# A head norm's four small transfers, moved from SyncE's queue to ScalarE's and GpSimd's

## The chip, the cores and the metric

The kernel runs on one core of a Trainium2 chip. The metric is the device time in microseconds of one execution; lower is better. Engines are named as the profile names them: PE (TensorE, the matrix multiplier; PEld is its weight load), DVE (VectorE), ACT (ScalarE), POOL (GpSimd) and SP (SyncE, which here only issues DMAs). An engine executes its instructions in the order in which they stand in its queue. A DMA is issued by an instruction in some engine's queue; if it has to wait for something, everything behind it in that queue waits too.

## What is computed

One layer of a hybrid decoder over 2048 tokens of width 1024, in float32. Two groups of token mixers run side by side on one input projection, their outputs go through one output projection, then a squared-ReLU MLP and a gated embedding follow. Cut to what matters here:

```python
def gated_head_norm(o, w, z):
    o = o * rsqrt(mean(o * o, axis=-1, keepdims=True) + EPS)
    return o * w * silu(z)

hn   = rms_norm(h, pre_mix_norm)
proj = einsum('btd,dc->btc', hn, w_in)
o_a  = gated_delta_rule_chunked(q_a, k_a, v_a, g_dec, beta)   # 4 heads of 128
o_a  = gated_head_norm(o_a, gdn_norm, z_gdn)
o_b  = hgrn2_chunked(silu(q_hg), k_b, i_hg, log_f)            # 4 heads of 128
o_b  = gated_head_norm(o_b, hgrn_norm, g_hg)
mix_out = einsum('btc,cd->btd', concat(o_a, o_b), w_out)
h = h + rms_norm(mix_out, post_mix_norm)
...   # MLP with its two norms, then the gated embedding
```

The change concerns `gated_head_norm`: 8 heads in each of 4 quarters of the tokens, 32 norms.

## The kernel before

Channels lie on the 128 partitions and tokens along the free axis, in quarters of 512 tokens (`QT`). A tile is `[128, 512]` float32. Weights and operands are split into two float32r parts, and a product is three matmuls.

**Order of the work.** The mixers are one loop over 132 `works` (for each quarter one product for the decays and 4 x 8 products for the heads). PE goes through them in the order in which the code is written (`manual_schedule` for PE), and so does SyncE within this loop. Each work is cut into 3 steps (`SPT`), and at each step a clock `tick()` resumes the generators that stand in an `agenda` at that step: `gdn_mixer` (the delta rule, names ending in `_g`) and `hgrn_mixer` (names ending in `_h`), one each per head. `A_STEPS` and `B_STEPS` are their lists of steps, counted from the head's first product; a head has 24 steps. The order on DVE, ACT and POOL in this part is not written out: the framework's planner sets it from the order of the code and from its own estimates of durations.

**The head norm.** Both mixers end in `finish`, which squares the head's output (`osq`), multiplies it by its gate (`og`) and calls `norm_steps`. This sums the squares over the partitions with two matmuls by a matrix of ones (L283, L284), so that each partition of a PSUM bank `nrm` holds all 512 sums. Then, in separate steps:

1. ACT copies one row of it (L286), and the row is stored to DRAM as `sd` (L288, 2 KB).
2. The row is loaded back as a block of 128 x 4, `m` (L291), so that the arithmetic is short.
3. DVE scales it (L293), POOL raises it to the power -0.5 (`rsqrt`, L172).
4. The block is stored to DRAM as `rd` (L297, 2 KB).
5. `spread_load` loads it, repeated on all partitions, as `rsb` (L257, 256 KB).
6. DVE multiplies `og` by the head's gain and `rsb` (L622), and `og` is stored to `mixd` (L624), from where the output projection's operands `mixT` are loaded (L341).

For the HGRN head these steps stand at 46, 48, 50, 52, 53, 54, 58 and 59 of `B_STEPS`, for the delta rule's head at 53, 55, 57, 59, 60, 61, 65 and 66 of `A_STEPS`. The last head of all has lists of its own (`A_LAST`, `B_LAST`).

All DMAs here are issued from SyncE. Its queue in the mixers also holds the weights: 512 KB raw loads and 1 MB stores to a cache in the first quarter, 1 MB loads from the cache afterwards (L197). Further, there are the delta rule's own round trips through DRAM (`ud` L709, `sys` L718, `xd` L752, `xn` L759, and `gf` L640), the squares of the next quarter's inputs (`xs` L495), and the MLP's weight sums (`wd` L1133, `sumd` L1144). POOL computes `rsqrt` for the norms, for the delta rule's keys (`rk`, on which DVE's L677 waits) and for the inputs, and clears `xn`. Its only DMAs are 16 that add the residual to the output projection's results (L1299), after the mixers.

`norm_steps` is also called for the embedding's norms (names ending in `_e`), and `spread_load` for others; these calls keep SyncE.

Of the kernel before, what the change touches and what calls it, by code (L numbers as in the profile page):

```python
# [20 lines left out]
P = 128  # L21
# [3 lines left out]
QT = 512  # L25
NQ = T // QT
NC = QT // P
# [69 lines left out]
def trunk(ctx, tc, x, xT, pT, vecs, w_in, w_ab, gdn_a_log, gdn_dt_bias, w_out, w_up, w_down,  # L97
          w_ple, w_gate, consts, out):
    nc = tc.nc
# [11 lines left out]
    def bank(name, pool=None):  # L111
        return (pool or pm).tile([P, QT], F32, tag="ps", name=name)
# [24 lines left out]
    def col(r):  # L137
        return cols[:, r : r + 1]
# [32 lines left out]
    def rsqrt(v):  # L171
        G.tensor_tensor(v, v, mhalf, ALU.pow)  # L172

    def split(t, eng, raw):

        S.activation(t[:, 0], raw, AF.Copy)  # L176
        eng.tensor_tensor(t[:, 1], raw, t[:, 0], ALU.subtract)  # L177
# [56 lines left out]
    def squares(acc, src, k, name, eng=V):  # L234

        if acc is None:
            acc = st.tile([P, QT], F32, tag="acc", name=f"acc_{name}", bufs=3)
            S.activation(acc, src, AF.Square)
        else:
            turns[0] += 1  # L240
            if pair[0] and turns[0] % 2:
                sq = st.tile([P, QT], F32, tag="late", name=f"sq_{name}_{k}")
            else:
                sq = st.tile([P, QT], F32, tag="sq", name=f"sq_{name}_{k}", bufs=1)
            S.activation(sq, src, AF.Square)  # L245
            eng.tensor_tensor(acc, acc, sq, ALU.add)  # L246
        return acc
# [4 lines left out]
        nc.sync.dma_start(rd.rearrange("o (p n) -> (o p) n", n=NC), m)  # L252
        return rd

    def spread_load(rd, name, pool=None, tag="rsb", bufs=2):
        rsb = (pool or st).tile([P, QT], F32, tag=tag, name=f"rsb_{name}", bufs=bufs)
        nc.sync.dma_start(rsb, rd.broadcast_to([P, QT]))  # L257
        return rsb

    def row_norm(acc, scale, eps, name):  # L260

        out = []
        for _ in norm_steps(acc, scale, eps, name, out.append):
            pass
        return out[0]
# [8 lines left out]
    yod = {q: [dr.tile([P, QT], F32, name=f"yod{q}_{d}") for d in range(KD)] for q in (0, 2, 3)}  # L274
    ple_r = [None] * NQ

    def norm_steps(acc, scale, eps, name, done, pool=None):

        hl = st.tile([P, 2, QT], F32R, tag="hl", name=f"hl_{name}", bufs=1)
        split(hl, V, acc)  # L280
        yield
        ps = bank(f"nrm_{name}", pool or pp)
        PE.matmul(ps, ones, hl[:, 0, :], start=True, stop=False)  # L283
        PE.matmul(ps, ones, hl[:, 1, :], start=False, stop=True)  # L284
        row = acc[0:1, :]
        S.activation(row, ps[0:1, :], AF.Copy)  # L286
        sd = dr.tile([1, QT], F32, name=f"sd_{name}")
        nc.sync.dma_start(sd, row)  # L288
        yield
        m = sm.tile([P, NC], F32, tag="m", name=f"m_{name}")  # L290
        nc.sync.dma_start(m, sd.rearrange("o (p n) -> (o p) n", n=NC))  # L291
        yield
        V.tensor_scalar(m, m, scale, eps, ALU.mult, ALU.add)  # L293
        rsqrt(m)
        yield
        rd = dr.tile([1, QT], F32, name=f"rd_{name}")
        nc.sync.dma_start(rd.rearrange("o (p n) -> (o p) n", n=NC), m)  # L297
        done(rd)

    def stage_ple(i, name):  # L300
# [91 lines left out]
    with ExitStack() as ectx:  # L392
        es = ectx.enter_context(tc.tile_pool(name="es", bufs=1))
        with tc.manual_schedule(engines={mybir.EngineType.SP, mybir.EngineType.Activation, mybir.EngineType.DVE}):
# [39 lines left out]
            ple[1] = ple1(V)  # L434
            x_r[0] = spread(ss, "x0")
            rsb = spread_load(x_r[0], "x0")
            load_xraw((4, 6))
            nc.sync.dma_start(cst[:, C_NEG:], consts[:, C_NEG:])
            done = []
# [23 lines left out]
    with mixers as mctx:  # L463
# [145 lines left out]
        def finish(q, h, pso, zt, extra, eps, n):  # L609

            og = st.tile([P, QT], F32, tag="late", name=f"og_{n}")
            sq = st.tile([P, QT], F32, tag="acc", name=f"osq_{n}", bufs=3)
            S.activation(sq, pso, AF.Square, scale=P ** -0.5)
            V.tensor_tensor(og, pso, zt, ALU.mult)
            if extra is not None:
                V.tensor_tensor(sq, sq, extra, ALU.add)
            rd = []
            yield from norm_steps(sq, 1.0, eps, n, rd.append)
            yield
            rsb = spread_load(rd[0], n)  # L620
            yield
            V.scalar_tensor_tensor(og, og, col(R_GNORM if h < 4 else R_HNORM), rsb, ALU.mult, ALU.mult)  # L622
            yield
            nc.sync.dma_start(mixd[q][h], og)  # L624
# [10 lines left out]
        def gdn_mixer(q, h, live):  # L635
# [181 lines left out]
            for c in range(NC):  # L817
# [20 lines left out]
                state[h] = s2  # L838
                yield
            yield from finish(q, h, pso, live.pop("z"), q2, EPS * EPS * P, n)  # L840

        def side(t, n, s, late):
# [17 lines left out]
        def hgrn_mixer(q, h, live):  # L860
# [101 lines left out]
            for c in range(NC):  # L962
# [4 lines left out]
                if c % 2:  # L967
                    yield
            yield from finish(q, 4 + h, pso, zt, None, EPS, n)


# [118 lines left out]
        def load_x(q):  # L1090

            rsb = spread_load(x_r[q], f"x{q}", m2, "rsx", 1)
            raws = {}

# [61 lines left out]
        for q in range(2):  # L1156
            at(0, norm_steps(accs[q], 1.0 / D, EPS, f"e{q}", partial(ple_r.__setitem__, q)),
               [4 * q + i for i in (0, 2, 4, 5, 6)])
# [302 lines left out]
    for j, (q, d) in enumerate(order):  # L1461
# [46 lines left out]
        acc = square_sums[q] = squares(square_sums[q], ps, d, f"o{q}")  # L1508
# [404 lines left out]
    rsb = {q: spread_load(ple_r[q], f"pg{q}", None, "acc", 3) for q in (0, 1)}  # L1913
    es, puts = {(q, 0): embedded(q, 0, rsb[q]) for q in (0, 1)}, []
    for half in range(2):
# [4 lines left out]
        for d in range(KD):  # L1920
# [4 lines left out]
            if d + 1 == KD and half == 0:  # L1925
                rsb = {q: spread_load(ple_r[q], f"pg{q}", None, "acc", 3) for q in (2, 3)}
# [65 lines left out]
```

## Time and profile before

| | |
|---|---|
| time, median of 3 runs | 2636.42 us (2636.26 to 2639.48) |
| the profiled execution: time, span | 2639.52 us, 2637.8 us |
| granted TensorE clock, mean | 0.999 |
| PE, PEld | 2602.5 us (99%), 2146.7 us (81%) |
| DVE, ACT, POOL | 1964.9 us (74%), 1464.5 us (56%), 137.7 us (5%) |
| DMA | 573.87 MB, mean 218 GB/s |
| DMA by queue, share of 16 engines | hardware queue 64.6%, software queue (POOL's) 1.0% |

A row of a group of instructions gives line, engine, operation, written tile <- read tiles, count, and durations (minimum/median/maximum in ns) or busy time. "A <- B: total, times, longest" is a wait: A's engine stood idle until B ended. `SPq` and `POOLq` are issues in these engines' queues; the time of an issue is the instruction's, not the transfer's. In a timeline a line begins with start and duration in us, and brackets give the idle time ahead of it and what ended it. The granted clock is a share of TensorE's full speed.

### The profile page before, as it was taken

The numbers are of one execution on the slowest core, as the hardware profiler recorded it, in microseconds if no ns is written. First come the engines' busy times: TensorE is split into PE (matmuls) and PEld (weight loads), VectorE is DVE, ScalarE is ACT, GpSimd is POOL, SyncE is SP. The second block draws the span as 40 slices with busy tenths as digits, with TensorE's granted clock in tenths as the row PEclk, the third lists the DMA queues.
The fourth block names the chain that finished last, engine by engine and source line by source line (L and its number), as shares of the span: only waits on it lengthen the run. The fifth ranks groups of instructions, "written<-read, shape, count | busy, mean of one in ns | idle before, by whom it ended". The sixth has DMA issues, their size and how long they took to land.

```text
span 2637.8 us, 43913 instructions
## 1 busy us (share of the span) xinstructions
PE 2602.5 (99%) x15593; PEld 2146.7 (81%) x15593; DVE 1964.9 (74%) x4032; ACT 1464.5 (56%) x2991; POOL 137.7 (5%) x147
## 2 busy tenths in 40 slices
PE   8999999999999999999999999999999999999999
PEld 6788888887878888877888888888888888888887
DVE  7778777776777777579988778767877765477776
ACT  7775655465556555566666455555455465565332
POOL 0000000000000000110000000001000001101000
PEclk9999999999999999999999999999999999999999
DMA  8877777767767675864675576665644375677663
GB/s 276 286 265 261 268 267 235 229 228 242 244 205 247 224 236 162 237 206 135 219 233 180 180 235 224 211 214 185 221 146 168 140 246 186 203 252 253 202 218 133
DMA packets 267788, 573.87 MB, mean 218 GB/s; under 512 B 55578, under 2 KB 60152, under 8 KB 250416
## 3 DMA queue, kind: packets, MB, share of 16 engines
q1 hardware_dynamic: 265264, 566.86, 64.6%
q0 software_dynamic: 2304, 4.20, 1.0%
q8 instruction: 123, 2.02, 0.3%
q14 instruction: 97, 0.79, 0.1%
HBM read 410.57 MB, written 160.37 MB: 216 GB/s over the span
## 4 chain that ended last, share of the span: by engine, by line
PE 68%; DVE 3%; DMA 3%; issue 2%; ACT 1%; SPq 0%; POOL 0%; DVEq 0%; ACTq 0%; POOLq 0%
PE d L1213 23%; PE u L1213 23%; PE mm L1179 9%; PE mmg L1213 7%; PE mmo L1062 1%; PE mme L203 1%; DMA yod<-yo 1%; DMA mixT<-mixd 0%; DVE t L177 0%; DVE acc_o L246 0%; DMA sys_g<-ud_g 0%; PE psc_g L832 0%; PE of_g L837 0%; PE of_g L836 0%; PE of_h L966 0%
## 5 line engine op out<-in xcount | busy, mean ns | idle before, releaser
L1179 PE MATMUL mm<-xt,w 128*128 128x512 f32 x3072 | 786.4, 401 | 1.2 <-DVE acc_vg L571 1.1
L1179 PEld LDWEIGHTS mm<-xt,w 128*128 128x128 f32 x3072 | 553.8, 189 | 107.4 <-issue 1.6
L1213 PE MATMUL d<-db,da 128*128 128x512 f32 x2688 | 612.9, 389 | 0.0
L1213 PE MATMUL u<-t,wu 128*128 128x512 f32 x2604 | 591.2, 389 | 0.0
L1213 PEld LDWEIGHTS d<-db,da 128*128 128x128 f32 x2688 | 504.5, 188 | 104.8
L1213 PEld LDWEIGHTS u<-t,wu 128*128 128x128 f32 x2604 | 488.7, 188 | 101.5
L230 DVE TENSOR_TENSOR db<-db 128x512 fp32r<-128x512 f32 x224 | 160.6, 717 | 58.2 <-ACT db L229 56.8
L1615 DVE TENSOR_TENSOR u<-u,u 128x512 f32<-128x512 f32 x224 | 150.4, 682 | 52.4 <-PE u L1213 50.9
L229 ACT ACTIVATE db<-db 128x512 fp32r<-128x512 f32 x224 | 141.0, 630 | 66.4 <-DMA db<-hid 62.0
L1213 PE MATMUL mmg<-h2T,wg 128*128 128x512 f32 (+1 forms) x792 | 174.7, 383 | 0.0
L1213 PEld LDWEIGHTS mmg<-h2T,wg 128*128 128x128 f32 x792 | 145.5, 188 | 29.1
L1658 ACT ACTIVATE u<-u 128x512 f32<-128x512 f32 x128 | 80.8, 631 | 153.2 <-DVE u L1615 152.2
L177 DVE TENSOR_TENSOR da<-da 128x512 fp32r<-128x512 f32 x128 | 94.1, 736 | 90.3 <-ACT da L176 88.3
L176 ACT ACTIVATE da<-da 128x512 fp32r<-128x512 f32 x128 | 80.7, 630 | 127.1 <-DMA da<-sumd 103.6
L1213 PE MATMUL mmo<-mixT,w_out 128*128 128x512 f32 x600 | 138.1, 390 | 2.7 <-DVE w_out L177 2.7
L1213 PEld LDWEIGHTS mmo<-mixT,w_out 128*128 128x128 f32 x600 | 112.3, 188 | 27.4 <-DVE w_out L177 4.0
L176 ACT ACTIVATE wu<-a 128x512 fp32r<-128x512 f32 x124 | 75.0, 623 | 54.5 <-DMA a<-in_w_up_dram 52.2
L177 DVE TENSOR_TENSOR wu<-a,wu 128x512 fp32r<-128x512 f32 x124 | 85.9, 695 | 7.9 <-ACT wu L176 7.5
L177 DVE TENSOR_TENSOR da<-dr,da 128x512 fp32r<-128x512 f32 x96 | 68.2, 711 | 23.6 <-ACT da L176 22.7
L1659 ACT ACTIVATE u<-u 128x512 f32<-128x512 f32 x128 | 80.4, 628 | 3.0
L246 POOL TENSOR_TENSOR acc_y<-acc_y,sq_y 128x512 f32<-128x512 f32 x28 | 38.5, 1375 | 758.9 <-ACT sq_y L245 758.9
L176 ACT ACTIVATE da<-dr 128x512 fp32r<-128x512 f32 x96 | 60.5, 630 | 28.9 <-DMA dr<-in_w_down_dram 23.9
(401 smaller groups left out, 3680.2 us busy)
## 6 DMA issues: line engine op xcount, KB each, us to landing
w<-cache_in SPq DMA_DIRECT2D x96, 1024.0 KB
db<-hid SPq DMA_DIRECT2D x224, 256.0 KB
cache_in<-w SPq DMA_DIRECT2D x32, 1024.0 KB
hid<-u SPq DMA_DIRECT2D x128, 256.0 KB
da<-sumd SPq DMA_DIRECT2D x128, 256.0 KB
a<-in_w_up_dram SPq DMA_DIRECT2D x124, 256.0 KB
hid<-ht SPq DMA_DIRECT2D x96, 256.0 KB
dr<-in_w_down_dram SPq DMA_DIRECT2D x96, 256.0 KB
```

The lines of the kernel that those rows point to most:

```text
L176: S.activation(t[:, 0], raw, AF.Copy)
L177: eng.tensor_tensor(t[:, 1], raw, t[:, 0], ALU.subtract)
L203: PE.matmul(ps, a, b, start=i == 0, stop=i == n - 1)
L229: S.activation(t[:, 0], plain(t), AF.Copy)
L230: V.tensor_tensor(t[:, 1], plain(t), t[:, 0], ALU.subtract)
L246: eng.tensor_tensor(acc, acc, sq, ALU.add)
L1062: PE.matmul(ps, w[:, term // 2, k, :], xin[q][k][:, term % 2, :], start=i == 0, stop=i == 3 * KD - 1)
L1179: PE.matmul(ps, *terms[i], start=i == 0, stop=i == nt - 1)
L1213: PE.matmul(ps, a, b, start=start, stop=stop)
L1615: V.tensor_tensor(c[new], c[old], ps, ALU.add)
L1658: S.activation(c[k], c[k], AF.Relu)
L1659: S.activation(c[k], c[k], AF.Square)
```

## The change

In the head norms of the mixers alone, four DMAs change their issuing engine: the row's store `sd` is issued by ScalarE, the block's load `m`, its store `rd` and the spread load `rsb` by GpSimd. Sizes, steps, buffers and arithmetic stay. Since ScalarE's and GpSimd's queues are ordered by the planner in this part, the place of these DMAs in their new queues is the planner's choice, while on SyncE it was the place in the code.

```diff
-    def spread_load(rd, name, pool=None, tag="rsb", bufs=2):
+    def spread_load(rd, name, pool=None, tag="rsb", bufs=2, queue=nc.sync):
         rsb = (pool or st).tile([P, QT], F32, tag=tag, name=f"rsb_{name}", bufs=bufs)
-        nc.sync.dma_start(rsb, rd.broadcast_to([P, QT]))
+        queue.dma_start(rsb, rd.broadcast_to([P, QT]))
         return rsb
...
-    def norm_steps(acc, scale, eps, name, done, pool=None):
-
+    def norm_steps(acc, scale, eps, name, done, pool=None, aside=False):
+
+        give, take = (nc.scalar, nc.gpsimd) if aside else (nc.sync, nc.sync)
...
         sd = dr.tile([1, QT], F32, name=f"sd_{name}")
-        nc.sync.dma_start(sd, row)
+        give.dma_start(sd, row)
         yield
         m = sm.tile([P, NC], F32, tag="m", name=f"m_{name}")
-        nc.sync.dma_start(m, sd.rearrange("o (p n) -> (o p) n", n=NC))
+        take.dma_start(m, sd.rearrange("o (p n) -> (o p) n", n=NC))
         yield
         V.tensor_scalar(m, m, scale, eps, ALU.mult, ALU.add)
         rsqrt(m)
         yield
         rd = dr.tile([1, QT], F32, name=f"rd_{name}")
-        nc.sync.dma_start(rd.rearrange("o (p n) -> (o p) n", n=NC), m)
+        take.dma_start(rd.rearrange("o (p n) -> (o p) n", n=NC), m)
         done(rd)
...
-            yield from norm_steps(sq, 1.0, eps, n, rd.append)
-            yield
-            rsb = spread_load(rd[0], n)
+            yield from norm_steps(sq, 1.0, eps, n, rd.append, aside=True)
+            yield
+            rsb = spread_load(rd[0], n, queue=nc.gpsimd)
```

## The prediction

> **What bounds the kernel now.** I read the page's busy times first, then the busy time by stretch, then who waited for whom, then the chain that ended last.
>
> ```profile
> span 2637.8 us, 43913 instructions
> PE 2602.5 (99%) x15593; PEld 2146.7 (81%) x15593; DVE 1964.9 (74%) x4032; ACT 1464.5 (56%) x2991; POOL 137.7 (5%) x147
> 90.00:1010.00 920.00, 909.49 (x7888) 752.24 (x7887) 700.90 (x2026) 531.75 (x1405) 53.10 (x61) 1.00 0.73 244
> 1010.00:1220.00 210.00, 202.19 (x1084) 164.81 (x1083) 151.73 (x255) 127.50 (x227) 18.71 (x20) 1.00 0.64 191
> ```
>
> The third and fourth lines are stretches: length, then busy us of PE, PEld, DVE, ACT and POOL, granted clock, DMA share, GB/s. TensorE is idle for 2637.8 - 2602.5 = 35.3 us in all. The changed norms run in the mixers (90 to 1010) and in the first part of the output projection (to 1093). There PE is idle for 920 - 909.5 = 10.5 us and 210 - 202.2 = 7.8 us. So 18.3 us, 0.7%, is all that a perfect result could remove, apart from what an idle stretch costs in clock afterwards.
>
> ```profile
> PE at_all L918 <- DVE acc_vg L572: 3.3, 1, 3.3
> PE mmo L1213 <- DVE w_out L177: 2.7, 3, 1.2
> 610.75 5.74 DMA rd_g<-m_g
> 616.56 4.56 DMA rsb_g<-rd_g
> 621.15 0.75 DVE og_g L622
> 624.05 1.10 PE at_all L918 x4
> 617.00 0.63 ACT L500 ACTIVATE xs<-xs 128x512 f32<-128x512 f32 x1 [2.01 <-DMA xs<-in_x_dram]
> 611.16 0.38 SPq L495 DMA_DIRECT2D xs<-in_x_dram  x1
> 620.00:625.00 5.00, 1.70 (x10) 1.46 (x9) 3.82 (x8) 1.33 (x4) 0.00 (x0) 0.91 1.01 393
> 625.00:630.00 5.00, 5.00 (x19) 4.01 (x19) 4.56 (x14) 2.24 (x5) 0.00 (x0) 0.74 0.65 202
> ```
>
> The first two lines are PE's waits (total, times, longest). The largest one in the mixers, 3.3 us before 624.05, is the end of a head norm: the chain's pieces (start, length) run through the norm's store rd_g, its spread load rsb_g and the multiplication L622, behind which the conv taps (acc_vg) stand on DVE. The ACT line shows a second delay just ahead of it: xs, issued on SyncE right after rd_g's store (611.16 behind 610.75), came 2.0 us late. The two stretches show the price after the gap: granted clocks of 0.91 and 0.74, which is 5 x 0.09 + 5 x 0.26 = 1.75 us.
>
> **The change part by part.** Per head norm four DMAs leave SyncE's queue: the row's store sd (to ScalarE), and the block's load m, its store rd and the spread load rsb (to GpSimd). There are 32 norms.
>
> ```profile
> L288 SPq DMA_DIRECT2D sd_h<-osq_h x16: 245/246/252, 156.6 to 1056.2; - x16
> L291 SPq DMA_DIRECT2D m_h<-sd_h x16: 319/322/1008, 161.3 to 1057.3; - x16
> L297 SPq DMA_DIRECT2D rd_h<-m_h x16: 319/332/463, 166.9 to 1061.7; - x16
> L257 SPq DMA_DIRECT2D rsb_h<-rd_h x16: 319/323/1589, 172.2 to 1064.7; - x16
> SPq L297 <- POOL m_g L172: 32.9, 10, 5.4
> SPq L197 <- PE mm L1179: 233.4, 59, 8.2
> DVE pr_g L730 <- DMA sys_g<-ud_g: 16.7, 11, 2.7
> DVE og_g L622 <- DMA rsb_g<-rd_g: 17.7, 11, 2.9
> ```
>
> *Removed from SyncE.* The four issues take 0.246 + 0.322 + 0.332 + 0.323 = 1.22 us (medians, ns in the rows; the sixteen g norms are taken as equal), so 39 us for 32, and with them go SyncE's waits for the norms, of which the row of m_g's store alone has 32.9 us. Almost none of it is on PE's path: SyncE spends 233.4 us waiting for PE to free weight buffers, so it is ahead with the weights. What it does reach is what stands behind a norm's wait: the delta rule's stores and loads (ud, sys; DVE waited 16.7 us for sys) and xs.
>
> *Added to ScalarE.* 32 issues. No issue from ScalarE is in this trace; the nearest row is SyncE's 0.246 us, so 8 us. ACT is busy for 531.75 of 920 us, so they fall into idle time: 0. If every one stood in PE's way, +8; that is the far end.
>
> *Added to GpSimd.* 96 issues. The nearest row is the same kind of DMA from that queue, in the output projection:
>
> ```profile
> L1299 POOL DMA_DIRECT2D yo<-in_xT_dram x16: 872/875/1347, 1098.6 to 1152.9; - x16
> DMA to landing us min/median/max: 4.0/7.8/12.6
> 550.15 1.01 POOL L172 TENSOR_TENSOR m_g<-m_g,mhalf 128x4 f32<-128x4 f32 x1 [3.91 <-DVE tail_g L651]
> 551.13 1.01 POOL L172 TENSOR_TENSOR rk_g<-rk_g,mhalf 128x4 f32<-128x4 f32 x1
> 800.14 1.01 POOL L172 TENSOR_TENSOR m_g<-m_g,mhalf 128x4 f32<-128x4 f32 x1 [3.91 <-DVE tail_g L651]
> 801.12 1.01 POOL L172 TENSOR_TENSOR rk_g<-rk_g,mhalf 128x4 f32<-128x4 f32 x1
> DVE cc_g L677 <- POOL rk_g L172: 15.2, 13, 1.6
> ```
>
> 96 x 0.875 = 84 us on an engine busy for 53 of 920 us: hidden as time. But GpSimd works in order and these DMAs wait for each other's landing, as SyncE's do now. Behind them stand the power rk_g, for which DVE already waits 15.2 us over 13 heads, and the clearing of xn_g. At 550 and 800 us, where a quarter of the tokens begins, the norm's power and rk_g come directly after each other. There rk_g can come to stand behind rd_g's issue, its landing and rsb_g's issue, 0.875 + 3.0 + 0.875 = 4.75 us (the 3.0 from the rows below). DVE's longest wait for rk_g, 1.6 us, shows how little its neighbours mind; of the 3.1 us left I let half reach PE, as DVE is busy for three quarters of the time: +3 for both places. The lower end is 0, the upper end is the slower rival below.
>
> *The chain itself.* The same four steps where DMA traffic is lighter (the last h norm), and the last g norm's effect:
>
> ```profile
> 1056.20 0.25 SPq L288 DMA_DIRECT2D sd_h<-osq_h  x1
> 1057.34 0.32 SPq L291 DMA_DIRECT2D m_h<-sd_h  x1
> 1061.67 0.32 SPq L297 DMA_DIRECT2D rd_h<-m_h  x1
> 1064.69 0.32 SPq L257 DMA_DIRECT2D rsb_h<-rd_h  x1
> 1067.72 0.75 DVE L622 SCALAR_TENSOR_TENSOR og_h<-og_h,cols,rsb_h 128x512 f32<-128x512 f32 x1 [1.11 <-DMA rsb_h<-rd_h]
> 606.37 0.32 SPq L197 DMA_DIRECT2D w<-cache_in  x1
> w<-cache_in SPq DMA_DIRECT2D x96, 1024.0 KB
> ```
>
> Here the links take 1.1 us, 4.3 us with the arithmetic behind m, 3.0 and 3.0 us, and the chain 11.5 us. At 610 us rd_g took 5.74 and rsb_g 4.56, with a weight load of 1 MB issued on the same queue at 606.37 before them. From another queue, I take the light links plus GpSimd's dearer issue (0.875 against 0.32 us, 0.55 more): rd_g + rsb_g = 7.1 us instead of 10.3, so 3.2 us earlier, enough for L622's wait. With xs freed as well, the whole 3.3 us gap goes, and its 1.75 us of clock: -5.0. The far end is that GpSimd's transfers land after 4.0 us or more, as yo's do (256 KB each and with an addition): then the two links take 8 us at the least and up to 25, and the gap stays or grows. I take the light links because m, rd and sd are 2 KB each.
>
> The Trainium skill (DMA: Bandwidth & Descriptors, Queues, rings and completion order) says that each DMA engine takes turns between the rings of its queues, packet by packet; the 5.74 us behind a megabyte against 3.0 us without one agrees with that, and by it the small transfers come forward. The same page (SWDGE vs HWDGE) gives GpSimd's path about 1 us to the first byte against 0.6 for SyncE and ScalarE; by that alone each link would be 0.4 us longer instead of my 0.55, and the sum would not move by 1 us. The page SBUF — State Buffer (Who interferes with whom) says that GpSimd cannot write descriptors while DVE runs a copy in its two-port mode; the 1.35 us at most of an issue in the row above shows no more than 0.5 us of that, and with it in each GpSimd issue one chain would take 1.4 us more.
>
> *The last g norm.* Its store makes SyncE wait, and the operand loads of the output projection stand behind it:
>
> ```profile
> 1083.31 0.32 SPq L297 DMA_DIRECT2D rd_g<-m_g  x1
> 1083.68 0.43 SPq L341 DMA_DIRECT2D mixT<-mixd  x1
> 1088.31 0.63 ACT L229 ACTIVATE mixT<-mixT 128x512 fp32r<-128x512 f32 x1 [3.15 <-DMA mixT<-mixd]
> 1101.63 11.22 PE L1213 MATMUL mmo<-mixT,w_out 128*128 128x512 f32 x48 [1.07 <-DVE w_out L177]
> ```
>
> ACT idles 3.15 us for that operand, is full afterwards, and splits w_out late, for which PE waits 1.07 us. Without the norm in its queue SyncE issues mixT earlier: -1.1. The other w_out waits, 2.7 - 1.07 = 1.6 us, I leave as they are. The rest of the mixers' idle time, 10.5 - 3.3 = 7.2 us, I count at 0, though the earlier ud and sys could take part of it, to -5.
>
> **Sum.** -5.0 - 1.1 + 3 = -3.1 us. The profiled execution took 2639.5 us (its span and 1.7 us around it), 3.1 above the median of 2636.4, so the sum gives 2636.4 against that execution's own time; carried to the median it is 2633.3.
>
> **The rivals.**
> - *Everything it speeds up is already covered, or something else ends at the same time.* PE's order is written out, but the planner orders DVE, ACT and now GpSimd's DMAs, so L622 may again stand ahead of the conv taps with its data late. For it: 17.7 us of waiting at L622 cost PE one gap of 3.3 us. Against it: that gap's two causes are both on SyncE's queue. Time: 2636.4. The Trainium skill (DMA: Bandwidth & Descriptors, Issuing engines are not separate DMA queues) would give this too: it says another issuing engine saves only the issue time.
> - *The delta rule gains as well.* ud and sys leave SyncE up to 5.4 us earlier (its longest wait for m_g), DVE's 16.7 us for sys and 17.7 us at L622 mostly go, and PE's other idle time goes with them: -5.0 - 1.1 - 5 with no loss on GpSimd, less 1 for what is left, is -10: 2626. Against it: few of PE's other waits name those lines.
> - *Slower: GpSimd's order.* If the spread load rsb_g, with its wait for rd_g's landing, is taken ahead of rk_g, DVE, in order, stands for the whole 4.75 us, and PE behind it; with 1.75 us of clock, as after the gap at 624, that is 6.5 us, at two places 13. In the other 14 heads the same order would cost some 0.3 us each in DVE's wait for rk_g, 4 in all. Less the gains of 6.1 us: +11, or +7 without the other heads; I take +9: 2645. It decides from 3 us of PE idle time at each of the two places, where the gains are used up.
>
> **How the numbers follow.** The time is told from no change at about 0.2%, 5.3 us. Chances: my forecast 0.36, covered 0.17, delta rule too 0.26, slower 0.21. Forecast and covered lie within 0.2%, but for their edges: same 0.47, faster 0.30, slower 0.23. The likeliest case alone reaches from 2630 to 2638. The range goes to the faster case, 2624, and to the slower one, 2646; outside it are GpSimd links of yo's length on one side, and the loss of all 18.3 us of idle time on the other.
>
> **What would show it.** After: PE's wait of 3.3 us near 624 gone and the clock there at 1.00; L622's waits for rsb_g under half of 17.7 us; mixT's load not behind a norm; no large new wait of DVE for rk_g; GpSimd's issues near 0.9 us. Wrong if DVE waits more for m_g, rsb_g or rk_g than now, or if the planner's new order of DVE and ACT opens other gaps at PE.

## The result: 5.2% slower, and the profile after

The changed kernel takes 2776.2 us (median of 4, 2766.1 to 2783.2), the kernel before 2637.0 us (median of 4): 1.0523 times as long, 95% interval 1.0486 to 1.0561. The forecast was 2633.3 us, the range 2624 to 2646. Of the changed kernel, the page's busy times and two stretches of the busy time (length, then PE, PEld, DVE, ACT and POOL, granted clock, DMA share, GB/s):

```profile
span 2781.4 us, 43850 instructions
PE 2640.6 (95%) x15593; PEld 2171.1 (78%) x15593; DVE 1961.6 (71%) x4032; ACT 1464.4 (53%) x2991; POOL 196.2 (7%) x243
90.00:1010.00 920.00, 829.60 (x6893) 679.56 (x6892) 616.26 (x1783) 472.70 (x1239) 91.77 (x126) 0.96 0.66 217
1360.00:2781.00 1421.00, 1415.67 (x6266) 1172.79 (x6264) 1049.48 (x1628) 742.71 (x1235) 58.36 (x44) 1.00 0.61 200
```

PE is idle for 2781.4 - 2640.6 = 140.8 us where it was 35.3. These 105.5 us more are most of the 143.6 us that the span grew; the other 38.1 us are the same 15593 matmuls at a lower mean clock (2640.6 against 2602.5 us busy; 0.980 against 0.999). The first stretch, all of it mixers, has 90.4 us idle against 10.5 and a clock of 0.96 against 1.00. From 1360 us on PE is idle for 5.3 us, at full clock. Who waited for whom, first one line of the kernel before that is needed for comparison, then the changed kernel (total, times, longest):

```profile
DVE og_h L622 <- DMA rsb_h<-rd_h: 5.5, 5, 1.9
```

```profile
PE at_all L919 <- DVE acc_vg L573: 60.9, 11, 13.7
PE nrm_g L284 <- ACT hl_g L176: 28.7, 7, 7.2
DVE og_g L623 <- DMA rsb_g<-rd_g: 83.1, 14, 11.2
DVE og_h L623 <- DMA rsb_h<-rd_h: 53.0, 11, 9.4
DVE m_g L294 <- DMA m_g<-sd_g: 21.9, 8, 5.2
DVE cc_g L678 <- POOL rk_g L172: 13.9, 10, 2.6
```

Lines from the norm on are one higher than before (the multiplication L622 is now L623). PE's one wait of 3.3 us for the value taps acc_vg (the convolution of the delta rule's values, three multiply-adds and a correction at the edge) has become eleven with 60.9 us. DVE's waits for the spread load rsb grew from 17.7 + 5.5 to 136.1 us. The wait for rk_g stayed.

The first long gap shows how. The timeline of the kernel before, rows of DVE and one of PE:

```profile
185.59 0.75 DVE L571 SCALAR_TENSOR_TENSOR acc_vg<-mm,cols,acc_vg 128x509 f32<-128x509 f32 x1 [1.01 <-ACT hist L568]
186.26 0.16 DVE L293 TENSOR_SCALAR m_g<-m_g 128x4 f32<-128x4 f32 x1
186.38 0.75 DVE L571 SCALAR_TENSOR_TENSOR acc_vg<-mm,cols,acc_vg 128x510 f32<-128x510 f32 x1
188.18 0.74 DVE L571 SCALAR_TENSOR_TENSOR acc_vg<-mm,cols,acc_vg 128x511 f32<-128x511 f32 x1
189.17 0.15 DVE L572 TENSOR_TENSOR acc_vg<-acc_vg,bound 128x3 f32<-128x3 f32 x1
189.82 0.68 PE L918 MATMUL at_all<-qk_h,keys_h 128*128 128x128 f32 x4 [1.11 <-ACT y_vg L577]
194.82 0.74 DVE L622 SCALAR_TENSOR_TENSOR og_g<-og_g,cols,rsb_g 128x512 f32<-128x512 f32 x1
```

The same norm in the changed kernel, timeline rows of DVE, POOL and PE, and then four stretches of 5 us (busy times, clock, DMA as above):

```profile
186.59 0.17 DVE L294 TENSOR_SCALAR m_g<-m_g 128x4 f32<-128x4 f32 x1 [3.64 <-DMA m_g<-sd_g]
189.11 0.61 POOL L298 DMA_DIRECT2D rd_g<-m_g  x1 [0.30 <-POOL m_g L172]
197.41 0.54 POOL L257 DMA_DIRECT2D rsb_g<-rd_g  x1 [7.36 <-DMA rd_g<-m_g]
202.42 0.75 DVE L623 SCALAR_TENSOR_TENSOR og_g<-og_g,cols,rsb_g 128x512 f32<-128x512 f32 x1 [10.86 <-DMA rsb_g<-rd_g]
203.09 0.74 DVE L572 SCALAR_TENSOR_TENSOR acc_vg<-mm,cols,acc_vg 128x509 f32<-128x509 f32 x1
205.87 0.74 DVE L572 SCALAR_TENSOR_TENSOR acc_vg<-mm,cols,acc_vg 128x511 f32<-128x511 f32 x1
207.11 1.19 PE L919 MATMUL at_all<-qk_h,keys_h 128*128 128x128 f32 x4 [13.70 <-DVE acc_vg L573]
```

```profile
195.00:200.00 5.00, 0.00 (x0) 0.00 (x0) 0.00 (x0) 0.00 (x0) 0.54 (x1) 0.67 0.52 93
200.00:205.00 5.00, 0.00 (x0) 0.00 (x0) 2.58 (x4) 0.00 (x0) 0.00 (x0) 0.50 0.44 111
205.00:210.00 5.00, 2.89 (x9) 2.54 (x10) 4.60 (x11) 3.27 (x7) 0.00 (x0) 0.50 0.78 256
210.00:215.00 5.00, 5.00 (x29) 4.20 (x28) 4.19 (x23) 4.05 (x11) 0.00 (x0) 0.97 0.71 242
```

Before, all three taps ran ahead of the multiplication, which found its data there, and PE waited 1.11 us. Now the multiplication is ahead of the taps, DVE stands idle for 10.86 us in front of it, the taps are late, and PE waits 13.7 us and then goes on at half clock. This is the rule, not one case: between 90 and 1300 us PE has 18 gaps of more than 2 us, and 15 of them, 92.3 of 101.5 us, come directly behind such a stand of DVE at a multiplication. The Trainium skill (TensorE: Matmul & The Clock Gate, What's actually happening) has the idle TensorE fall to 4/8 of its clock after a window of about 3.4 us; the 0.50 of these rows agrees.

Nothing in the change names that order: the planner set it. Counted over the two instruction sequences, PE's order is the same, and the 32 multiplications stand 9.5 places earlier on DVE on the mean (h 8.1, g 10.9, up to 20), while the scalings of m moved by 0.8 (h) and 6.7 (g). On DVE a multiplication stood a median of 26 (h) and 21 (g) places behind its norm's scaling, now 17.5 and 13; in three norms it is 2. The transfers did not become shorter by as much. Medians after the end of the row's copy, read from the timelines (us):

| | m issued | scaling | rd issued | rsb issued | multiplication |
|---|---|---|---|---|---|
| h, before | 1.7 | 5.1 | 6.6 | 13.1 | 18.5 |
| h, after | 2.1 | 5.4 | 7.0 | 12.6 | 19.0 |
| g, before | 2.7 | 10.3 | 11.7 | 15.2 | 20.1 |
| g, after | 2.8 | 7.9 | 9.8 | 13.6 | 19.0 |

So the theory, A: the planner's new order of DVE is the cost. The rival, B: GpSimd's queue (its waits, or slower transfers) is. In what follows "held order" means that extra edges without a semaphore keep an engine's instructions in a listed order (the other engines' orders stay the planner's):

```diff
+    for text in ORDERS:
+        wanted = ["I-" + n for n in zlib.decompress(base64.b64decode(text)).decode().split(",")]
+        for a, b in zip(wanted, wanted[1:]):
+            tc.add_manual_dep(traced[b], a, mybir.DependencyInfo(mybir.DependencyClass.NoSync, ...), reason="order")
```

### The profile page after: what moved, and what is told of

The parts are those of the page before. It is cut to its first block, busy times and chain, and to the rows that moved or that the text cites. A ratio compares the mean times of both kernels' runs of the same rounds, so it can differ in the third digit from the quotient of the medians.

```text
span 2781.4 us, 43850 instructions
## 1 busy us (share of the span) xinstructions
PE 2640.6 (95%) x15593; PEld 2171.1 (78%) x15593; DVE 1961.6 (71%) x4032; ACT 1464.4 (53%) x2991; POOL 196.2 (7%) x243
## 4 chain that ended last, share of the span: by engine, by line
PE 51%; issue 2%; DVE 1%; DMA 1%; ACT 1%; POOL 0%; SPq 0%; DVEq 0%; ACTq 0%; POOLq 0%
PE d L1214 22%; PE u L1214 22%; PE mmg L1214 6%; PE mme L203 1%; DMA yod<-yo 0%; DMA yo<-in_xT_dram 0%; DVE t L177 0%; DVE acc_o L246 0%; DMA b<-h1d 0%; DVE b L1370 0%; DMA rsb_g<-rd_g 0%; ACT yo L1508 0%; DVE b L1373 0%; ACT sq_o L245 0%; DVE w_out L177 0%
## 5 line engine op out<-in xcount | busy, mean ns | idle before, releaser
L1180 PE MATMUL mm<-xt,w 128*128 128x512 f32 x3072 | 808.8, 410 | 3.1 <-DVE acc_vg L572 1.6
L1180 PEld LDWEIGHTS mm<-xt,w 128*128 128x128 f32 x3072 | 570.2, 194 | 114.2 <-ACT w L176 2.0
```

The costliest lines, as they stand in the source:

```text
L1180: PE.matmul(ps, *terms[i], start=i == 0, stop=i == nt - 1)
```

## Experiments: order against queues

**New queues, VectorE's order of before.** The edit is the loop above in the changed kernel, with the 4032 DVE instructions of before.

> The changed kernel's queues, with every DVE instruction held in the order that it has in the kernel before (order only, no waits added). Theory A (the planner's new DVE order, in which the 32 multiplications by rsb stand 9.5 places earlier on average, makes DVE stand for transfers that take as long as before): 2625 to 2645 us, DVE's waits for rsb back from 136 us to under 35. Theory B (GpSimd's queue itself, its waits and its transfers): at least 2700 us, with the waits for rsb still over 80 us.

Measured 2671.4 us, 1.0131 (1.0110 to 1.0152), with waits for rsb of 40 us. About 105 of the 139 us go; 34 remain, so both figures are above what A gave and below B's.

**Old queues, VectorE's new order.** The same loop in the kernel before, with the changed kernel's list; no transfer moves.

> The queues of the kernel before, with every DVE instruction held in the order that it has in the changed kernel. Theory A: 2740 to 2800 us, as slow as the changed kernel or more so, with waits of over 100 us for rsb. Theory B: 2630 to 2650 us, no change from before.

Measured 2811.7 us, 1.0659 (1.0640 to 1.0678), above A's range. The order alone, with every DMA on SyncE, is slower than the change: its waits for rsb are 161 us against 136. B as the main cause falls. That the new queues help at this order, by 2811.7 - 2776.2 = 35 us, is not shown: ScalarE's order was left to the planner, and in this trace 504 of its 2923 operations (table loads left out) stand at another place than in the changed kernel, with 76 table loads of 1.28 us instead of 68.

**Only the multiplications early.** The kernel before, with DVE's order of before in all but the 32 multiplications. The list that is held was made like this, in outline:

```python
for x in multiplications:
    order.remove(x)
    order.insert(order.index(scaling[x]) + places_after[x], x)
```

> The queues of before and VectorE's order of before in all but the 32 multiplications: each stands as many places behind its norm's scaling of m as in the changed kernel (median 17.5 instead of 26 for h, 13 instead of 21 for g; on the mean 6.7 places earlier, up to 20). No transfer and no other VectorE instruction is moved. Theory, the early multiplication is what costs: 2700 to 2790 us, VectorE's waits for rsb over 100 us. Rival, the other 350 or so moved VectorE instructions matter as much: 2640 to 2690 us.

Measured 2755.0 us, 1.0432 (1.0405 to 1.0459), as A gave. This kernel's waits, and one of its gaps in the timeline:

```profile
PE nrm_g L283 <- ACT hl_g L176: 42.1, 7, 8.3
PE at_all L918 <- ACT y_vg L578: 33.2, 5, 8.0
DVE og_h L622 <- DMA rsb_h<-rd_h: 67.5, 14, 10.2
DVE og_g L622 <- DMA rsb_g<-rd_g: 51.2, 12, 8.1
796.34 0.75 DVE L622 SCALAR_TENSOR_TENSOR og_h<-og_h,cols,rsb_h 128x512 f32<-128x512 f32 x1 [9.09 <-DMA rsb_h<-rd_h]
798.33 0.63 ACT L176 ACTIVATE hl_g<-osq_g 128x512 fp32r<-128x512 f32 x1 [7.43 <-DVE osq_g L616]
799.01 0.79 PE L283 MATMUL nrm_g<-hl_g,ones 128*128 128x512 f32 x1 [6.92 <-ACT hl_g L176]
```

32 instructions of 0.75 us, moved 6.7 places on the mean, cost 115 us. For 118.7 us DVE stands in front of them, and what it does next (the squares osq_g, from which ACT and DVE make the parts of hl_g, and the taps) reaches PE late. One rival is left by the edit: the planner, free on ScalarE, gave 271 of its 2923 operations another place. The trace decides: 13 of PE's 16 gaps over 2 us between 90 and 1300 us, 73.6 of 84.8 us, come directly behind a stand of DVE at a multiplication.

**The multiplications where the code issues them**, in both kernels, the planner free otherwise.

```diff
-            V.scalar_tensor_tensor(og, og, col(...), rsb, ALU.mult, ALU.mult)
+            tc.keep_in_program_order(V.scalar_tensor_tensor(og, og, col(...), rsb, ALU.mult, ALU.mult))
```

> The new queues and a free planner, but the 32 multiplications by the spread norm stand where the program issues them (on the mean 0.1 places later than before for h, 7.3 later for g, instead of 8.1 and 10.9 earlier). Theory, the early multiplication is the cost: VectorE's waits for rsb fall from 136 us to under 40, and the time to between 2640 and 2680 us. Rival, the other moved instructions (the scalings of m, ScalarE's order) carry as much: over 2700 us.

> The kernel before with the 32 multiplications where the program issues them, on the mean 2.5 (h) and 6.8 (g) places later; no transfer is moved. Theory: VectorE's waits for rsb (17.7 and 5.5 us) fall to under 10 and the gap of 3.3 us before 624 goes: 2625 to 2637 us. Rival: a later multiplication makes the square, the product and the copy after it late at PE: 2640 to 2660 us.

With the new queues 2693.2 us, 1.0202 (1.0187 to 1.0218): 83 us better than the change, but over the 2680 that A gave at most. The waits for rsb are down to 26 us; in their place DVE now waits for m, whose scaling the planner still takes early:

```profile
DVE m_g L294 <- DMA m_g<-sd_g: 31.3, 9, 5.8
DVE og_h L623 <- DMA rsb_h<-rd_h: 14.8, 5, 5.0
```

In the kernel before 2642.4 us, 1.0015 (1.0004 to 1.0026), at the edge of no change, and not the gain that A gave. Its waits:

```profile
DVE og_g L622 <- DMA rsb_g<-rd_g: 2.0, 2, 1.5
PE at_all L918 <- DVE acc_vg L572: 2.2, 1, 2.2
```

Nearly all of the 23.2 us that DVE waited for rsb is gone, and no time with it. Either those waits were covered, or a later multiplication costs as much elsewhere: the time lies in the rival's range, and DVE's wait for sys_g grew from 16.7 to 23.2 us. This run doesn't separate the two.

## Experiments: what the queues themselves cost

**The row's store alone, and the spread load alone**, planner free. The edits keep `nc.sync` for the other DMAs:

```diff
-        give, take = (nc.scalar, nc.gpsimd) if aside else (nc.sync, nc.sync)
+        give, take = (nc.scalar, nc.sync) if aside else (nc.sync, nc.sync)
```

> Only the row's store sd goes to ScalarE; m, rd and rsb stay on SyncE. The planner moves the multiplications by 0.7 places on average. Theory A: 2630 to 2645 us, no change. Theory B: the same, since GpSimd issues nothing. A slowdown of over 10 us would mean that ScalarE's issue is a cost of its own.

> Only the spread load rsb goes to GpSimd. The planner moves the multiplications by 2.9 places on average, a third of the full change. Theory A: about a quarter of the loss, 2645 to 2680 us. Theory B: half of the waits on GpSimd's queue are there (the wait for rd), so 2680 to 2720 us.

The row's store 2651.7 us, 1.0051 (1.0033 to 1.0070): 14 us for 32 issues of 0.2 us, where both theories gave none. By the expectation that would be a cost of ScalarE's issue itself, but the table below gives only some 3 us to the moved store with the orders held. The multiplications moved by 0.7 places, but 429 of DVE's 4032 instructions and 129 of ScalarE's 2923 operations stand at another place, and DVE's waits for rsb rose to 44.2 us. The spread load 2674.1 us, 1.0137 (1.0119 to 1.0155), inside A's range: its multiplications stand 3.8 (h) and 1.9 (g) places earlier. As the table below shows, about half of these 37 us is not order but the queue itself.

**VectorE's and ScalarE's orders of before**, with all four DMAs on their new queues, and with each part alone.

> The new queues, with all 4032 VectorE instructions and all 2833 ScalarE operations held in the order of before (only ScalarE's 32 new issues come in between). With VectorE's order alone held the time was 2671.4 us, 34 us over before. Theory: those 34 us are ScalarE's new order (145 of its rows stood elsewhere): 2632 to 2647 us. Rival: the links themselves take longer on the new queues (the wait for m, the issue behind it on GpSimd's queue), so each multiplication waits 3 us longer at the place it had: 2660 to 2680 us, with VectorE's waits for rsb near the 28.4 and 11.6 us of the run before.

> Only the row's store on ScalarE's queue, with VectorE's and ScalarE's orders of before. With the planner free this change alone gave 2651.7 us, 14 us over before. Theory, the order of ScalarE and VectorE costs it: 2632 to 2642 us. Rival, the store on ScalarE's queue costs it (its issues, or its landing later): 2647 to 2656 us.

> Only the block's load and its store on GpSimd's queue, VectorE and ScalarE in the order of before. Theory, the spread load carries the 25 us that remain: 2636 to 2648 us here. Rival, these two carry them: 2652 to 2668 us. If neither alone gives more than 10 us, it is their being behind one another on one queue.

> Only the spread load on GpSimd's queue, VectorE and ScalarE in the order of before. Of the change with both orders held 25 us remain (2664.1 against 2639.0 us). Theory, the spread load carries them (on GpSimd's queue it waits for its norm's store, up to 8 us, with the split of rk_g and the next load of m behind it): 2652 to 2668 us. Rival, the load of m and the store behind it carry them: 2636 to 2646 us.

| orders of DVE and ACT held | us | ratio |
|---|---|---|
| all four moved | 2664.1 | 1.0094 (1.0072 to 1.0116) |
| row's store on ScalarE | 2642.8 | 1.0011 (1.0002 to 1.0021) |
| block's load and store on GpSimd | 2644.7 | 1.0015 (1.0006 to 1.0025) |
| spread load on GpSimd | 2659.2 | 1.0077 (1.0060 to 1.0095) |

In the first row the rival's time holds, not the theory's: of the 34 us, ScalarE's order is worth some 9 (1.0131 against 1.0094, with intervals that just overlap), and 25 us belong to the queues. The row's store ends just above its theory's 2642, far from its rival; the other two rows are as their theories gave. The parts add up within their intervals (0.11 + 0.15 + 0.77 = 1.03%, against 0.94%), and three quarters is the spread load. The same norm, first in the kernel before and then with the spread load alone on GpSimd, both timelines:

```profile
863.47 0.32 SPq L257 DMA_DIRECT2D rsb_g<-rd_g  x1
866.80 0.75 DVE L622 SCALAR_TENSOR_TENSOR og_g<-og_g,cols,rsb_g 128x512 f32<-128x512 f32 x1 [1.91 <-DMA rsb_g<-rd_g]
```

```profile
874.94 0.60 POOL L257 DMA_DIRECT2D rsb_g<-rd_g  x1 [3.55 <-DMA rd_g<-m_g]
881.79 0.75 DVE L623 SCALAR_TENSOR_TENSOR og_g<-og_g,cols,rsb_g 128x512 f32<-128x512 f32 x1 [7.63 <-DMA rsb_g<-rd_g]
885.48 1.19 PE L919 MATMUL at_all<-qk_h,keys_h 128*128 128x128 f32 x4 [5.45 <-DVE acc_vg L573]
```

From issue to multiplication 3.3 us become 6.9, at the same place in DVE's order, and PE gets a gap of 5.5 us that was not there. This is a long one: over all multiplications that waited, the median is 4.6 us before (16) and 5.6 us with the spread load on GpSimd (21). With DVE's order the same and the spread load still on SyncE, the kernels of the table's second and third row have 5.1 (23) and 5.3 us (16), so of this difference 0.3 to 1.0 us is the queue's.

**The multiplication a little later.** First, the new queues with DVE's and ScalarE's orders of the pinned kernel before; then five multiplications only, those of g norms directly ahead of the value taps, put directly behind them (3 to 6 places), in three kernels. In outline:

```python
for x in five:
    order.remove(x)
    order.insert(last_value_tap[x], x)
```

> The new queues, with VectorE's and ScalarE's orders of the kernel with the pinned multiplications (2642.4 us on the old queues: the multiplications stand 2.5 places later for h and 6.8 for g, nothing else of weight moved). Theory, the 25 us that remain with the orders of before are the multiplications' waits for rsb (55.7 us instead of 23.2): those waits fall under 25 us and the time to 2638 to 2652 us. Rival, they are waits of something else in the chain (the scaling of m, the split of rk_g): 2655 to 2670 us.

> The new queues with the orders of before, but for five of VectorE's 32 multiplications: those g norms' that stand directly ahead of the value taps (acc_vg), for which the convolution's attention part at_all waits at PE, stand directly behind them, 3 to 6 places later. Theory: the 25 us that remain with the orders of before come mainly from these places (PE's gaps of 4.6 and 4.2 us there, and the clock behind them): 2640 to 2652 us and no wait of PE for acc_vg over 2 us. Rival, the spread load's later landing costs at many small places, or the clock is lost elsewhere: 2655 to 2668 us.

> The kernel before with the same five multiplications behind the taps, its queues and its other order unchanged. It removes the gap of 3.3 us near 624 that the prediction let the change remove. Theory, the gap and its clock were worth 5 us: 2630 to 2636 us against about 2638 of before. Rival, PE's gap only moves (the multiplication is late for its own norm's user, or the gap's time is taken by the next transfer): 2636 to 2645 us.

> The row's store on ScalarE's queue, the block's load and store on GpSimd's, the spread load back on SyncE's, with the orders of before and the five multiplications behind the taps: the change without the two things that cost. Theory: 2632 to 2644 us, no different from before, as each of the two moves alone cost 3 to 5 us and the five places give that back. Rival, the two moves together make the chain late as the spread load does: 2648 to 2662 us.

The pinned orders gave 2659.5 us, 1.0071 (1.0055 to 1.0087), in the rival's range and only 4.5 us better than the orders of before, though DVE's waits for rsb fell from 55.7 to 14.6 us. So most of these waits cost little, unless the later multiplications cost as much elsewhere. Two multiplications do not move in that order, and there PE's gaps, the only two over 2 us between 90 and 1300 us, stay, as its timeline shows:

```profile
636.70 1.19 PE L919 MATMUL at_all<-qk_h,keys_h 128*128 128x128 f32 x4 [5.00 <-DVE acc_vg L573]
889.63 0.68 PE L919 MATMUL at_all<-qk_h,keys_h 128*128 128x128 f32 x4 [4.26 <-DVE acc_vg L573]
```

The five moved gave 2654.7 us, 1.0060 (1.0048 to 1.0072): 9 of the 25 us, between the theory's 2652 and the rival's 2655. Three gaps of PE over 2 us are left there between 90 and 1300 us. One is the same thing elsewhere, as the first two rows of that kernel's timeline show; before another, DVE stood for the block's load m_g, as the last two show:

```profile
1090.14 0.75 DVE L623 SCALAR_TENSOR_TENSOR og_h<-og_h,cols,rsb_h 128x512 f32<-128x512 f32 x1 [6.08 <-DMA rsb_h<-rd_h]
1092.15 0.50 PE L285 MATMUL nrm_g<-hl_g,ones 128*128 128x512 f32 x1 [4.55 <-DVE hl_g L177]
505.06 0.17 DVE L294 TENSOR_SCALAR m_g<-m_g 128x4 f32<-128x4 f32 x1 [3.86 <-DMA m_g<-sd_g]
512.21 0.86 PE L919 MATMUL at_all<-qk_h,keys_h 128*128 128x128 f32 x4 [2.60 <-DVE acc_vg L573]
```

A late spread load of an h norm holds up hl_g, and with it PE. I did not move those places, and the three gaps have 10.5 us together, so where the last 16 us come from is argued from these rows, not shown.

In the kernel before the five moves gave 2637.7 us against 2639.1: 0.9997 (0.9987 to 1.0006), no change, as the rival gave. The gap near 624 shrank to half:

```profile
624.53 0.68 PE L918 MATMUL at_all<-qk_h,keys_h 128*128 128x128 f32 x4 [1.67 <-DVE acc_vg L572]
```

The change without its spread load, with these places mended, took 2649.9 us, 1.0038 (1.0025 to 1.0051): the theory's 2644 is missed, and the rival's range holds it. The interval still contains the 0.26% that row store and block cost one by one; whether they cost more together stays open, as the profiled execution was the fastest of the six (2642.5 us) and does not show it. No version that was run is faster than the kernel before.

## Why the prediction was wrong, step by step

- *What bounds the kernel*: right. At most 18.3 us could be won, and there was far more to lose. I kept in view what a gap costs PE, but not how near DVE's order is to many such gaps.
- *Removed from SyncE*: right as far as the traces show. The 39 us of issues left, and SyncE is still ahead with the weights: it waits 407.9 us for PE to free their buffers, 233.4 before.
- *Added to ScalarE*: 0.20 us an issue instead of 0.246. As time it is nearly hidden: with the orders held the move costs 0.11%, some 3 us, inside 0 to +8.
- *Added to GpSimd*: the issues were over-priced, and the harm was put in the wrong place. The rows of the changed kernel, each by its source line:

```profile
L289 ACTq DMA_DIRECT2D sd_h<-osq_h x16: 200/201/469, 158.8 to 1188.9; - x16
L292 POOL DMA_DIRECT2D m_h<-sd_h x16: 537/537/764, 164.0 to 1193.3; - x16
L298 POOL DMA_DIRECT2D rd_h<-m_h x16: 606/606/622, 167.8 to 1199.2; - x16
DMA to landing us min/median/max: 1.7/3.6/8.7
L257 POOL DMA_DIRECT2D rsb_h<-rd_h x16: 536/538/646, 173.8 to 1201.3; - x16
DMA to landing us min/median/max: 3.4/4.4/7.1
```

  0.54 to 0.61 us an issue, 54 us for 96, not 84. The rk_g that I priced at +3 (and the slower rival at two places) did not come: DVE waits 13.9 us for it, 15.2 before. With the orders held, most of the queues' cost is the spread load's. The first row also shows how much the mixers grew: from its first to its last issue 1030 us, where the kernel before has 900.
- *The chain itself*, -5.0: this step failed, in two ways. The links were taken from the place with the lightest traffic: rd and rsb at 3.0 us with 0.55 for the issue, 7.1 together. Their landing medians are 3.6 and 4.4, 8.0, and at the first gap 8.3 and 5.0. With DVE's and ScalarE's orders held, the way from the end of the row's copy to the multiplication became longer, on the mean 21.3 us instead of 19.7, not 3.2 shorter. And the multiplication was assumed to keep its place in DVE's order. It did not, and this is the large term: 1.0523 with the planner free less 1.0094 with the orders held is 4.3%, 113 us. Nor was the gain there to be had in the kernel before: 21 us fewer waits for rsb, by pinning, brought nothing, and halving the gap at 624 nothing that can be measured.
- *The last g norm*, -1.1: the opposite came. PE's wait for w_out behind ScalarE is 6.9 us in the changed kernel, one wait, in place of 1.07; ahead of it DVE stood 6.55 us at the last multiplication.
- *The rivals*: "covered" named the mechanism, a planner that puts L622 ahead of the taps with its data late, and priced it at 0; it is the term that was mis-sized. The reason given against it, that the gap's causes are on SyncE's queue, speaks of one gap and not of the eleven that a new order opens. Of the signs of being wrong, more waiting for rsb_g and new gaps at PE by the planner's new order are what happened. "The delta rule gains as well" came in the wait and not in the time: with both orders held DVE's wait for sys_g fell from 16.7 to 10.7 us, in a kernel that is 0.94% slower.
- *The pages cited*: the Trainium skill (DMA: Bandwidth & Descriptors, Issuing engines are not separate DMA queues) says that another issuing engine saves only the time of the issue. That the way to the multiplication did not become shorter with the orders held agrees with it. The 2636.4 that I drew from it left the order out. An estimate from the same page (Latency and other measured facts, 1 against 0.6 us to the first byte) made a link 0.4 us longer on GpSimd's path; the 0.3 to 1.0 us measured for the spread load, 0.27 of it in the issue, contain it.

That the planner takes the multiplication early because it reckons the transfers shorter on emptier queues is argued: the runs show the order and its price, not the planner's reasons.

## What to carry to other kernels

Where a planner orders the engines, moving a transfer to another queue can also change the order of engines that it doesn't touch, as each of the three moves with a free planner did here: compare the instruction order of all engines before and after, and hold the old one, before reading anything into the time. An in-order engine that stands at one late load delays everything behind it, so a consumer of a round trip through DRAM should not be moved ahead of work that the bound engine needs sooner. In the kernel before, moving it later still gained nothing. A wait that the trace shows on an engine off the path can be worth nothing; price it by the gap that it opens at the bound engine.

## What the runs showed of the hardware that was not expected

- A gap of 13.7 us costs PE beyond itself: the granted clock was still 0.50 in the stretch in which PE went on (205 to 210 us), and 0.97 in the next. Over the whole kernel the matmuls took 38 of the 144 us longer at the lower clock.
- The 256 KB spread load, with the same orders on DVE and ScalarE, reached the multiplications that waited for it 0.3 to 1.0 us later (medians) from GpSimd's queue than from SyncE's, and its move alone cost 0.77%.
- A 2 KB DMA's issue takes 0.54 to 0.61 us on GpSimd, and the 256 KB spread load's no more (0.54 to 0.60), against 0.88 for the 256 KB adding ones; the row's store takes 0.20 on ScalarE against 0.25 on SyncE.
